# Two low PSUM banks for the output projection and both FFN layers, and the last merged tile added on VectorE

## The chip, the cores and the metric

The kernel runs on one core of one Trainium2 chip. The metric is the device time of one execution in microseconds (us). TensorE (PE) does the matmuls and transposes; VectorE (DVE), ScalarE (ACT) and GpSimd (POOL) do the elementwise work; SyncE (SP) issues most of the DMA loads and stores. TensorE's results land in PSUM, which has eight banks here, each as wide as one 128x512 fp32 tile. TensorE's weight loads stand apart in the profile as PEld.

## The reference

Two batches, `x_prompt` and `x_sample`, both 1024 tokens by 1024 channels, go through one encoder layer with the same weights:

```python
proj = x @ w_in                       # q, k, v of A and of B, gates ga and gb
ya = mixer_a(qa, ka, va) @ w_branch_a # dilated window attention, 12 heads
yb = neighbourhood_attention(qb, kb, vb, rpb) @ w_branch_b
merged = sigmoid(ga + b_gate[0]) * ya + sigmoid(gb + b_gate[1]) * yb
x = layer_norm(alpha * x + merged @ w_out)
hid = square(relu(x @ w_ff1 + b_ff1)) # 4096 wide
x = layer_norm(alpha * x + hid @ w_ff2 + b_ff2)
```

## The kernel before

The program takes the batches one after the other and goes through the same stages for each: transposes of the input and the V columns, q and k and attention A, attention B and the gates, the merge of the two branches, the output projection with the first layer norm, FFN1, FFN2, the second layer norm. Every product of two fp32 matrices is three matmuls: each operand is split into a rounded high part and the low remainder (names that end in `h` and `l`, or 0 and 1), and high x high, high x low and low x high are summed in one bank. One such triple stands on lines L107 to L109, and the subtraction that makes a low part on L103.

A scheduler sets the order of the instructions on each engine from the tiles that they read and write, and from the pools from which the tiles come; the function names and loops of the code alone don't. Each engine then runs its own list strictly in order. A tile waits for the last reader of the tile that had its place before it.

Merge: for each of eight 128-channel tiles `nt` and each half `h` of the tokens, branch A goes into a PSUM tile `py0` and branch B into `py1` (pool `pga`, six banks). VectorE multiplies each by its gate (`sg`, L766), GpSimd adds the two (L767), ScalarE rounds the sum to `bh` (L768), and VectorE takes the low part `bl` (L103).

Output projection: for each half `nh` of the output channels and each half `h` of the tokens, four token tiles `i` take 24 matmuls each, so a group (nh, h) is 96 matmuls in four banks. With nh = 0 the loop over the eight k tiles is outside and the four tiles alternate. `z` is the residual: VectorE adds the finished bank to it (L881), and only then is the bank free. The tiles `wor`, `woh`, `wol` are the projection's weights; `w1t` and `w1b` are the first FFN1 weights, which SyncE loads in the same stretch, and which ScalarE and VectorE split (`oh`, `ol`, and `o` for a piece of `w1b`).

FFN1 runs a Strassen-like scheme in 16 jobs; the first four (`EARLY`) start while the transposes of the second half of the layer norm's output are still coming. Its PSUM tiles are `px`, `pz` and `py`. FFN2 runs the products of a like scheme into four long-lived `px` tiles and short-lived `pt` and `pr` tiles; `acc` is its sum in SBUF. At the end of the first batch VectorE adds the last `px` tiles to `acc`, normalises, and the second batch's input transposes (`pt`, L214) and V products (`psv`) start.

Where the PSUM tiles of before lie: transposes `pt` from the layer norm to FFN2 on banks 0 and 1; the projection's four `pso` on 2, 5, 4, 3; FFN1's and FFN2's `px` on the same four; `pz` and `py`, then `pr`, on 7 and 6. In the merge the last `py0` is on bank 2 and the last `py1` on bank 5.

Of the kernel before, what the change touches and what calls it, by code (L numbers as in the profile page):

```python
# [9 lines left out]
F32 = mybir.dt.float32  # L10
F32R = mybir.dt.float32r
AF = mybir.ActivationFunctionType
ALU = mybir.AluOpType
PSUM = bass.MemoryType.PSUM
# [4 lines left out]
P = 128  # L19
T = 1024  # L20
D = 1024
KT = D // P
# [59 lines left out]
def encoder_kernel(ctx, tc, xs, w_in, b_gate, w_a, w_b, w_out, rpb, ln1_g, ln1_b, w1, b1, w2, b2,  # L82
                   ln2_g, ln2_b, ident_d, rope_d, maska_d, maskb_d, outs):
    nc = tc.nc
# [185 lines left out]
    for b, x in enumerate(xs):  # L270
# [7 lines left out]
        pst = pool("ps_t", 2, space=PSUM)  # L278
# [475 lines left out]
        for nt in range(KT):  # L754
            ns = slice(nt * P, (nt + 1) * P)
            wu = wunit([w_a[:, ns], w_b[:, ns]])
            sg = [sgp.tile([P, T], F32, name=f"sg{s}", tag=f"sg{s}") for s in range(2)]
            for s in range(2):
                nc.sync.dma_start(sg[s], gd[b][s, nt])
                nc.scalar.activation(sg[s], sg[s], AF.Sigmoid)  # L760
            for h in range(2):
                hs = slice(512 * h, 512 * (h + 1))
                py = [pga.tile([P, 512], F32, name=f"py{s}", tag=f"py{s}") for s in range(2)]
                for s, (k0, k1) in enumerate(((0, 2), (2, 6))):
                    mmT(py[s], wu, abt[0][:, :, hs], abt[1][:, :, hs], k0, k1, k0)
                    nc.vector.tensor_tensor(sg[s][:, hs], sg[s][:, hs], py[s], op=ALU.mult)  # L766
                nc.gpsimd.tensor_tensor(sg[0][:, hs], sg[0][:, hs], sg[1][:, hs], op=ALU.add)  # L767
                nc.scalar.copy(mT[h][0][:, nt], sg[0][:, hs])  # L768
                sub(nc.vector, mT[h][1][:, nt], sg[0][:, hs], f(mT[h][0][:, nt]))
        pga.release()  # L770
# [14 lines left out]
        zp = pool("z", 4, side="right")  # L785
        ttp = pool("tt", 2, side="right")
        z0p = pool("z0", 4, side="right")
        pst = pool("ps_t2", 2, space=PSUM)
        pso = pool("ps_o", 4, space=PSUM)

        def split(oh, ol, src, eng):
            nc.scalar.copy(oh, src)  # L792
# [68 lines left out]
        for nh in range(2):  # L861
            wo = []
            for k in range(KT):
                raw = wrw.tile([P, 512], F32, name="wor", tag="wraw")
                nc.sync.dma_start(raw, w_out[k * P:(k + 1) * P, nh * 512:(nh + 1) * 512])
                wh = wop.tile([P, 512], F32R, name="woh", tag="woh")
                wl = wop.tile([P, 512], F32R, name="wol", tag="wol")
                split(wh, wl, raw, nc.vector)
                wo.append((wh, wl))
            for h in range(2):  # L870
                pss = [pso.tile([P, 512], F32, name="pso", tag="pso") for _ in range(4)]
                order = [(k, i) for k in range(KT) for i in range(4)]
                if nh == 1:
                    order.sort(key=lambda o: o[1])
                for k, i in order:
                    cs = slice(i * P, (i + 1) * P)
                    mm3(pss[i], mT[h][0][:, k, cs], mT[h][1][:, k, cs], *wo[k], k == 0, k == KT - 1)
                    if k < KT - 1:
                        continue
                    it = 4 * h + i  # L880
                    nc.vector.scalar_tensor_tensor(zs[it][:, nh], in0=zs[it][:, nh], scalar=ALPHA, in1=pss[i],  # L881
                                                   op0=ALU.mult, op1=ALU.add)
                    if nh == 1:
                        normalise(zs[it])
                        if it > 1:
                            follow(it - 2)
# [20 lines left out]
        sp_ = pool("w1s", 1)  # L907
        c11p = pool("c11", 4)
        psx = pool("ps_x", 4, space=PSUM)
        psy = pool("ps_y", 1, space=PSUM)  # L910
        psz = pool("ps_z", 1, space=PSUM)
        NP = FF // 256
        EARLY = 4

# [11 lines left out]
        def job_a(p, top):  # L926

            o = w1_ops(top, nc.vector)
            px = psx.tile([P, 512], F32, name="px", tag="px")
            prod(px, [t[:, :4] for t in o], xb[1], True)  # L930
            pl, tag = ((psz, "pz"), (psy, "py"))[p % 2 if p < EARLY else 0]
            pz = pl.tile([P, 512], F32, name=tag, tag=tag)
            prod(pz, [t[:, 4:] for t in o], xb[2], True)
            c11 = c11p.tile([P, 512], F32, name="c11", tag="c11")
            nc.scalar.copy(c11, px)  # L935
            nc.vector.tensor_tensor(c11, c11, pz, op=ALU.add)
            return px, c11
# [13 lines left out]
        def job_b(p, top, px, c11):  # L951
            bot = bots.pop(p)
            ss = sp_.tile([P, 4, 4, P], F32, name="ss", tag="ss")
            s2, s1, s3, s4 = (ss[:, i] for i in range(4))
            a11, a12, a21, a22 = top[:, :4], top[:, 4:], bot[:, :4], bot[:, 4:]
            nc.vector.tensor_tensor(s1, a21, a22, op=ALU.add)
            sub(nc.vector, s2, s1, a11)
            sub(nc.vector, s3, a11, a21)
            sub(nc.vector, s4, a12, s2)
            o65 = w1_ops(ss[:, 0:2].rearrange("p i k c -> p (i k) c"), nc.vector)  # L960
            o73 = w1_ops(ss[:, 2:4].rearrange("p i k c -> p (i k) c"), nc.vector)
            o4 = [opq.tile([P, 4, P], F32R, name=f"o4{s}", tag=f"o4{s}") for s in range(2)]
            split(*o4, a22, nc.vector)

            if p + 1 < NP:
                tops[p + 1] = w1_top(p + 1)
                bots[p + 1] = w1_bot(p + 1)
            residual_load(p - EARLY)
            relu2(c11, c11, 2 * p)
            put(p, 1, c11)  # L970
            u2, u3, p5 = (pup.tile([P, 512], F32, name=n, tag=n) for n in ("u2", "u3", "p5"))
            prod(px, [t[:, :4] for t in o65], xb[6], False)
            nc.scalar.copy(u2, px)
            py = psy.tile([P, 512], F32, name="py", tag="py")
            prod(py, [t[:, 4:] for t in o65], xb[5], True)
            nc.scalar.copy(p5, py)
            prod(px, [t[:, :4] for t in o73], xb[7], False)
            nc.scalar.copy(u3, px)
            prod(py, [t[:, 4:] for t in o73], xb[3], False)
            c12, c21, c22, h1, h2, h3, h4 = (htp.tile([P, 512], F32, name="ht", tag="ht") for _ in range(7))  # L980
            nc.vector.tensor_tensor(c12, u2, py, op=ALU.add)
            relu2(c12, c12, 2 * p)
            nc.vector.tensor_tensor(c22, u3, p5, op=ALU.add)
            relu2(c22, c22, 2 * p + 1)
            prod(px, o4, xb[4], False)
            relu2(c21, px, 2 * p + 1)

            put(p, 4, c22)
            put(p, 2, c21)
            nc.vector.tensor_tensor(h1, c12, c22, op=ALU.add)  # L990
            put(p, 5, h1)
            sub(nc.vector, h2, h1, c11)
            put(p, 6, h2)
            sub(nc.vector, h3, c11, c12)
            put(p, 7, h3)
            sub(nc.vector, h4, c21, h2)
            put(p, 3, h4)
# [26 lines left out]
        for p in range(NP):  # L1024
            top = tops.pop(p)
            job_b(p, top, *(early[p] if p < EARLY else job_a(p, top)))
            residual(p - EARLY)
        psz.release()
        psy.release()
        psx.release()  # L1030
        for q in (rsp, htp, pup, opq, opp, awp, c11p, sp_, bop, xbp):
            q.release()
# [19 lines left out]
        w2r = pool("w2r", 2, side="right")  # L1052
        jkp = pool("junk", side="right")
        psx = pool("ps_x", 4, space=PSUM)
        psr = pool("ps_r", 2, space=PSUM)
        nch = NP // 4
        px = [None] * 4

# [5 lines left out]
        for c in range(nch):  # L1064
# [34 lines left out]
            def product(m, t):  # L1099

                if m == 1:
                    px[t] = psx.tile([P, 512], F32, name="px", tag="px")
                if m in (1, 6, 7, 4):
                    ps = px[t]
                else:
                    pl, tag = ((pst, "pt"), (psr, "pr"))[t % 2]
                    ps = pl.tile([P, 512], F32, name=tag, tag=tag)
                cs = slice(t * P, (t + 1) * P)
                for u in range(2):
                    o = ops[m, u]  # L1110
                    for q in range(2):
                        mm3(ps, o[:, 0, q, cs], o[:, 1, q, cs], o[:, 2, q], o[:, 3, q], m not in (6, 7, 4) and u + q == 0,
                            u + q == 2, skip=True)
                for s_ in {1: (0,), 2: (0,), 6: (1,), 5: (1, 3), 3: (1,), 7: (3,), 4: (2,)}[m]:
                    a = acc[s_ // 2][:, t, s_ % 2]
                    nc.vector.tensor_tensor(a, a, ps, op=ALU.add)
                if last and (m == 3 or m == 4 and b + 1 == len(xs)):
                    finish(m == 4, t)
# [9 lines left out]
            if last:  # L1128
                for t in range(4):
                    product(7, t)  # L1130
                    product(4, t)
        psr.release()
        psx.release()
        pst.release()
        for q in (jkp, w2r, hrp, w2a, w2b, padp, ac0p):
            q.release()
        if b + 1 == len(xs):
# [42 lines left out]
```

## Time and profile before

| | before |
|---|---|
| device time, three runs, us | 3073.8, 3064.63, 3077.58 (median 3073.8) |
| profiled execution: time, span, us | 3073.11, 3071.3 |
| PE busy | 2925.7 us, 95% |
| VectorE busy | 1857.7 us, 60% |
| ScalarE busy | 1450.0 us, 47% |
| GpSimd busy | 954.8 us, 31% |
| mean DMA rate over the span | 153 GB/s |

The span is the profiled execution from first to last instruction. Busy time counts an instruction from start to end. TensorE's matmuls overlap: one of 128x512 is shown as 0.39 us, but the next starts 0.23 us after it at the full granted clock. A bracket at the end of a row gives the time for which the engine stood idle before it and the instruction that ended the wait. PEclk is the TensorE clock that was granted, 1.00 for 2.4 GHz and 0.50 for 1.2 GHz.

### The profile page before, as it was taken

To read this page: it belongs to the slowest core of one execution; us is meant where nothing else is said; L and a number is where in the kernel's file an instruction comes from. 1 tells how busy PE (TensorE), PEld (TensorE's weight loads), DVE (VectorE), ACT (ScalarE), POOL (GpSimd) and SP (SyncE) were. 2 spreads that over 40 slices of the span, in tenths; PEclk is the share of its full clock that TensorE was granted. 3 is DMA by queue.
4 is the path that set the end of the run, shared out by engine and by line. 5 is a ranking of instruction groups with operands and counts; after the bars stand their busy time and mean duration, and the time that the engine had idled before them with its cause. 6 is when DMAs were issued, how large, how long until landed. Compare 5 with 4: busy or idle time off the path is not lost. (4 is left out here: it accounts for less than half of the span.)

```text
span 3071.3 us, 39485 instructions
## 1 busy us (share of the span) xinstructions
PE 2925.7 (95%) x13965; PEld 2413.5 (79%) x13965; DVE 1857.7 (60%) x3448; ACT 1450.0 (47%) x2640; POOL 954.8 (31%) x768
## 2 busy tenths in 40 slices
PE   9999999898998999899899999999989999989997
PEld 8887887787776887688797888777878777867886
DVE  2166667545477555888731666685454676558777
ACT  3165755454274554333431656554542745543333
POOL 4665633414014000233242645334140140003332
PEclk9999999999999999999999999999999999999999
DMA  8622235555456547544353222355544565465442
GB/s 254 237 79 80 85 107 154 160 173 154 153 177 226 170 138 258 184 151 138 98 197 109 78 85 76 107 154 163 173 151 159 177 227 164 150 251 167 151 137 82
DMA packets 390662, 471.25 MB, mean 153 GB/s; under 512 B 28424, under 2 KB 270008, under 8 KB 390208
## 3 DMA queue, kind: packets, MB, share of 16 engines
q1 hardware_dynamic: 363968, 430.45, 43.7%
q10 hardware_dynamic: 26496, 38.28, 3.5%
q8 instruction: 110, 1.80, 0.2%
q14 instruction: 88, 0.72, 0.1%
HBM read 321.50 MB, written 147.52 MB: 153 GB/s over the span
## 5 line engine op out<-in xcount | busy, mean ns | idle before, releaser
L107 PE MATMUL pmm<-bh,whi 128*128 128x512 f32 x1152 | 466.1, 405 | 6.8 <-DVE kz L103 4.9
L108 PE MATMUL pmm<-bh,wlo 128*128 128x512 f32 x1152 | 464.0, 403 | 0.0
L109 PE MATMUL pmm<-bl,whi 128*128 128x512 f32 x1152 | 463.1, 402 | 0.0
L103 POOL TENSOR_TENSOR wlo<-wraw,whi 128x512 fp32r<-128x512 f32 (+1 forms) x176 | 225.6, 1294 | 438.9 <-ACT whi L198 383.8
L107 PEld LDWEIGHTS pmm<-bh,whi 128*128 128x128 f32 x1152 | 219.0, 190 | 49.4 <-DVE kz L103 5.9
L400 ACT ACTIVATE smk<-smk,nm 128x256 f32<-128x256 f32 (+4 forms) x320 | 162.3, 508 | 194.7 <-DVE nm L399 176.9
L109 PEld LDWEIGHTS pmm<-bl,whi 128*128 128x128 f32 x1152 | 218.9, 190 | 42.8
L108 PEld LDWEIGHTS pmm<-bh,wlo 128*128 128x128 f32 x1152 | 219.0, 190 | 41.0
L103 POOL TENSOR_TENSOR ts<-rw,rw 128x1024 f32<-128x1024 f32 x12 | 33.7, 2811 | 671.8 <-DMA rw<-in_w_ff_dram 298.2
L792 ACT CAST bh<-hr 128x1024 fp32r<-128x1024 f32 x56 | 58.8, 1050 | 331.2 <-PE px L109 171.5
L103 DVE TENSOR_TENSOR ptl<-pt,pth 128x512 fp32r<-128x512 f32 (+3 forms) x224 | 125.6, 569 | 67.0 <-ACT pth L711 44.2
L107 PE MATMUL psv<-wv,bh 128*128 128x384 f32 (+1 forms) x384 | 138.6, 362 | 1.5 <-ACT wv L295 1.3
L108 PE MATMUL psv<-wv,bl 128*128 128x384 f32 (+1 forms) x384 | 139.2, 363 | 0.3 <-DVE bl L103 0.3
L109 PE MATMUL psv<-wv,bh 128*128 128x384 f32 (+1 forms) x384 | 138.0, 361 | 1.3 <-POOL wv L103 1.2
L103 POOL TENSOR_TENSOR qs<-r,qs 64x512 fp32r<-64x512 f32 x80 | 114.8, 1435 | 62.2 <-ACT qs L423 57.8
L103 DVE TENSOR_TENSOR vt<-psv,vt 128x384 fp32r<-128x384 f32 (+1 forms) x48 | 28.8, 602 | 165.1 <-ACT vt L351 165.1
L792 ACT CAST oh<-ss 128x1024 fp32r<-128x1024 f32 x64 | 67.2, 1053 | 123.2 <-DVE ss L103 93.5
L103 DVE TENSOR_TENSOR bh<-hr,bh 128x1024 fp32r<-128x1024 f32 x56 | 80.9, 1445 | 61.4 <-ACT bh L792 61.1
L198 ACT CAST whi<-wraw 128x512 fp32r<-128x512 f32 (+1 forms) x176 | 97.5, 596 | 42.2 <-DMA wraw<-in_w_in_dram 36.1
L107 PE MATMUL pso<-woh,bh 128*128 128x512 f32 x256 | 104.3, 407 | 12.7 <-DVE sg L766 12.7
L107 PE MATMUL px<-bh,oh 128*128 128x512 f32 x256 | 104.4, 408 | 9.6 <-ACT c L935 4.4
L108 PE MATMUL px<-bh,ol 128*128 128x512 f32 x256 | 104.1, 406 | 4.7 <-DVE ol L103 4.5
(281 smaller groups left out, 8360.2 us busy)
## 6 DMA issues: line engine op xcount, KB each, us to landing
hr<-hidd SPq DMA_DIRECT2D x112, 512.0 KB
hidd<-ht SPq DMA_DIRECT2D x192, 256.0 KB
wraw<-in_w_in_dram SPq DMA_DIRECT2D x144, 256.0 KB
rw<-in_w_ff_dram SPq DMA_DIRECT2D x64, 512.0 KB
w1t<-in_w_ff_dram SPq DMA_DIRECT2D x40, 512.0 KB
gd<-gt ACTq DMA_DIRECT2D x32, 512.0 KB
sg<-gd SPq DMA_DIRECT2D x32, 512.0 KB
w1b<-in_w_ff_dram SPq DMA_DIRECT2D x32, 512.0 KB
```

Source lines behind the costliest of these rows:

```text
L103: eng.tensor_tensor(out, a, b, op=ALU.subtract)
L107: nc.tensor.matmul(out, ah, bh, start=start, stop=False, skip_group_check=skip)
L108: nc.tensor.matmul(out, al, bh, start=False, stop=False, skip_group_check=skip)
L109: nc.tensor.matmul(out, ah, bl, start=False, stop=stop, skip_group_check=skip)
L198: nc.scalar.copy(hi[:, ks], raw[:, :k])
L400: nc.scalar.activation(pr[:, e0:e1], pr[:, e0:e1], AF.Exp, bias=nm, scale=1.0, accum_out=den)
L792: nc.scalar.copy(oh, src)
```

## The change

First, the last merged tile (`nt` = 7) adds its two gated branches on VectorE instead of GpSimd: four instructions in all, two per batch. Second, PSUM is laid out anew from the output projection on. A pool `psl` of two banks, 0 and 1, is opened first and kept until the end of the batch; `low(0)` and `low(1)` are its tiles (`pl0`, `pl1`). They take the projection's token tiles i = 0 and 1, then FFN1's `pz` and `py`, then FFN2's `pr`. The transposes' pool `pst` lies on banks 2 and 3, the projection's two `pso` on 4 and 5, `px` on 4, 7, 6, 5. In the next batch the first transposes lie on banks 2 and 3, which before belonged to `px` tiles and now to short-lived `pt` tiles.

```diff
@@ branch merge
-                nc.gpsimd.tensor_tensor(sg[0][:, hs], sg[0][:, hs], sg[1][:, hs], op=ALU.add)
+                eng = nc.vector if nt == KT - 1 else nc.gpsimd
+                eng.tensor_tensor(sg[0][:, hs], sg[0][:, hs], sg[1][:, hs], op=ALU.add)
@@ output projection
+        psl = pool("ps_l", 1, space=PSUM)
+
+        def low(i):
+            return psl.tile([P, 512], F32, name=f"pl{i}", tag=f"pl{i}")
+
         pst = pool("ps_t2", 2, space=PSUM)
-        pso = pool("ps_o", 4, space=PSUM)
+        pso = pool("ps_o", 2, space=PSUM)
...
-                pss = [pso.tile([P, 512], F32, name="pso", tag="pso") for _ in range(4)]
+                pss = [low(i) if i < 2 else pso.tile([P, 512], F32, name="pso", tag="pso") for i in range(4)]
@@ FFN1
-        psy = pool("ps_y", 1, space=PSUM)
-        psz = pool("ps_z", 1, space=PSUM)
...
-            pl, tag = ((psz, "pz"), (psy, "py"))[p % 2 if p < EARLY else 0]
-            pz = pl.tile([P, 512], F32, name=tag, tag=tag)
+            pz = low(p % 2 if p < EARLY else 0)
...
-            py = psy.tile([P, 512], F32, name="py", tag="py")
+            py = low(1)
@@ FFN2
-        psr = pool("ps_r", 2, space=PSUM)
...
-                    pl, tag = ((pst, "pt"), (psr, "pr"))[t % 2]
-                    ps = pl.tile([P, 512], F32, name=tag, tag=tag)
+                    ps = low(t // 2) if t % 2 else pst.tile([P, 512], F32, name="pt", tag="pt")
...
-        psr.release()
         psx.release()
         pst.release()
+        psl.release()
```

The scheduler makes a new order from this. Up to the end of the branch products of the first batch the order of TensorE is the same. TensorE at the start of the first batch's output projection, before (`py1` is the last branch product, `woh` and `wol` the weights, `bh0` and `bl0` the merged tile of the first half of the tokens):

```order
L109 MATMUL py1_8010<-ab1_7444,whi_7968 128x512
L107 MATMUL pso_8127<-woh_8081,bh0_7502 128x512
L108 MATMUL pso_8127<-woh_8081,bl0_7503 128x512
L109 MATMUL pso_8127<-wol_8082,bh0_7502 128x512
L107 MATMUL pso_8128<-woh_8081,bh0_7502 128x512
```

and now:

```order
L109 MATMUL py1_8010<-ab1_7444,whi_7968 128x512
L107 MATMUL pl0_8130<-woh_8084,bh0_7502 128x512
L108 MATMUL pl0_8130<-woh_8084,bl0_7503 128x512
L109 MATMUL pl0_8130<-wol_8085,bh0_7502 128x512
L107 MATMUL pl1_8131<-woh_8084,bh0_7502 128x512
```

The first tile was on bank 2 and the second on bank 5, both of which the merge had just used; now the two are on banks 0 and 1, and TensorE runs 23 matmuls into these before it turns to banks 4 and 5 (`pso_8132`, `pso_8133`).

VectorE from the end of the merge to the first tiles of the projection, before (`sg` the gates and the merged sum, `ol` and `o41` low parts of FFN1 weights, `z` the residual; `pso_8127` to `pso_8130` are the four banks of the first group):

```order
L766 TENSOR_TENSOR sg1_7979<-sg1_7979,py1_7985 128x512
L766 TENSOR_TENSOR sg0_7978<-sg0_7978,py0_8009 128x512
L103 TENSOR_TENSOR bl0_7503<-sg0_7978,bh0_7502 128x512
L766 TENSOR_TENSOR sg1_7979<-sg1_7979,py1_8010 128x512
L103 TENSOR_TENSOR bl1_7505<-sg0_7978,bh1_7504 128x512
L103 TENSOR_TENSOR ol_8969<-w1t_8966,oh_8968 128x1024
L103 TENSOR_TENSOR ol_9004<-w1t_9001,oh_9003 128x1024
L103 TENSOR_TENSOR o41_9135<-w1b_9119,o40_9134 128x512
L103 TENSOR_TENSOR ol_9039<-w1t_9036,oh_9038 128x1024
L881 SCALAR_TENSOR_TENSOR z_8063<-z_8063,pso_8127 128x512
L881 SCALAR_TENSOR_TENSOR z_8064<-z_8064,pso_8128 128x512
```

and now:

```order
L766 TENSOR_TENSOR sg1_7979<-sg1_7979,py1_7985 128x512
L768 TENSOR_TENSOR sg0_7978<-sg0_7978,sg1_7979 128x512
L766 TENSOR_TENSOR sg0_7978<-sg0_7978,py0_8009 128x512
L103 TENSOR_TENSOR bl0_7503<-sg0_7978,bh0_7502 128x512
L766 TENSOR_TENSOR sg1_7979<-sg1_7979,py1_8010 128x512
L768 TENSOR_TENSOR sg0_7978<-sg0_7978,sg1_7979 128x512
L103 TENSOR_TENSOR bl1_7505<-sg0_7978,bh1_7504 128x512
L103 TENSOR_TENSOR ol_8966<-w1t_8963,oh_8965 128x1024
L103 TENSOR_TENSOR ol_9001<-w1t_8998,oh_9000 128x1024
L103 TENSOR_TENSOR o41_9132<-w1b_9116,o40_9131 128x512
L888 SCALAR_TENSOR_TENSOR z_8066<-z_8066,pl0_8130 128x512
L888 SCALAR_TENSOR_TENSOR z_8067<-z_8067,pl1_8131 128x512
```

The two additions (now L768) stand between the multiplications. The first `z` still stands behind `o41`, the low part of `w1b`; one later `ol` has gone behind two of the `z`. TensorE's second group of 96 begins with the bank that the first `z` sets free, in both orders, and the second batch has the same order here.

VectorE at the end of the first batch, before (`acc` FFN2's sum in its last normalisation, `pt_13628` and `pt_13635` the first transposes of the second batch):

```order
L1116 TENSOR_TENSOR acc1_11457<-acc1_11457,px_13081 128x512
L236 TENSOR_TENSOR acc0_11456<-acc0_11456,bb2_13019 128x1024
L247 SCALAR_TENSOR_TENSOR acc1_11457<-acc1_11457,rs2_13793,bb2_13019 128x1024
L241 BN_AGGR mv_13810<-bst_13811 128x2
L243 TENSOR_SCALAR rs_13803<-mv_13798 128x1
L246 SCALAR_TENSOR_TENSOR acc1_11457<-acc1_11457,mv_13798,g2_13017 128x1024
L240 BN_STATS bst_13823<-acc1_11457 128x6
L103 TENSOR_TENSOR bl0_13604<-pt_13628,bh0_13603 128x4x128
L103 TENSOR_TENSOR bl0_13604<-pt_13635,bh0_13603 128x4x128
```

and now:

```order
L1116 TENSOR_TENSOR acc1_11452<-acc1_11452,px_13073 128x512
L236 TENSOR_TENSOR acc0_11451<-acc0_11451,bb2_13011 128x1024
L103 TENSOR_TENSOR bl0_13596<-pt_13620,bh0_13595 128x4x128
L240 BN_STATS bst_13803<-acc1_11452 128x6
L240 BN_STATS bst_13815<-acc1_11452 128x6
L103 TENSOR_TENSOR bl0_13596<-pt_13627,bh0_13595 128x4x128
L247 SCALAR_TENSOR_TENSOR acc1_11452<-acc1_11452,rs2_13785,bb2_13011 128x1024
L243 TENSOR_SCALAR rs_13795<-mv_13790 128x1
L246 SCALAR_TENSOR_TENSOR acc1_11452<-acc1_11452,mv_13790,g2_13009 128x1024
```

The two `bl0` that free the first two transpose banks have moved ahead of part of the normalisation, but still stand behind the addition of the last `px` and L236.

## Rows read from the trace of the kernel before

**Rows 1.** The page: busy us, share of the span, instructions, by engine.

```profile
PE 2925.7 (95%) x13965; PEld 2413.5 (79%) x13965; DVE 1857.7 (60%) x3448; ACT 1450.0 (47%) x2640; POOL 954.8 (31%) x768
```

**Rows 2.** Waits of TensorE: us in total, times, longest.

```profile
PE pt L107 <- ACT bh L792: 25.8, 3, 12.1
PE pso L107 <- DVE sg L766: 12.7, 4, 5.2
...
PE px L108 <- DVE ol L103: 4.5, 4, 1.1
PE px L107 <- ACT c L935: 4.4, 2, 2.6
...
PE pz L107 <- DVE c L936: 3.3, 2, 2.3
PE py L107 <- DVE c L936: 3.1, 2, 1.6
```

**Rows 3.** Timeline of TensorE, 763 to 796: start, us, line, operation, [idle before].

```profile
763.26 0.39 PE L109 MATMUL py<-ab,whi 128*128 128x512 f32 x1
768.87 0.80 PE L107 MATMUL pso<-woh,bh 128*128 128x512 f32 x1 [5.22 <-DVE sg L766]
...
777.34 0.40 PE L108 MATMUL pso<-woh,bl 128*128 128x512 f32 x1
...
795.52 0.39 PE L107 MATMUL pso<-woh,bh 128*128 128x512 f32 x1
```

**Rows 4.** Windows: stretch, length, engines' busy time, PEclk, DMA share, GB/s.

```profile
768.80:777.30 8.50, 7.29 (x16) 5.28 (x17) 1.99 (x4) 1.24 (x2) 2.11 (x2) 0.50 1.01 339
777.30:788.50 11.20, 11.20 (x51) 9.20 (x50) 2.45 (x2) 2.73 (x3) 0.00 (x0) 1.00 1.11 345
963.20:972.00 8.80, 8.62 (x28) 6.37 (x29) 8.77 (x11) 6.76 (x12) 3.43 (x2) 0.81 0.61 191
1531.30:1542.20 10.90, 7.52 (x28) 6.57 (x29) 10.85 (x15) 4.83 (x10) 8.46 (x6) 0.53 0.72 239
```

**Rows 5.** Timeline of VectorE, 767 to 796.

```profile
767.53 1.28 DVE L766 TENSOR_TENSOR sg<-sg,py 128x512 f32<-128x512 f32 x2
...
773.65 0.69 DVE L103 TENSOR_TENSOR bl<-sg,bh 128x512 fp32r<-128x512 f32 x1 [2.04 <-ACT bh L768]
...
788.53 0.69 DVE L103 TENSOR_TENSOR o<-w1b,o 128x512 fp32r<-128x512 f32 x1 [5.30 <-ACT o L792]
...
793.68 2.05 DVE L881 SCALAR_TENSOR_TENSOR z<-z,pso 128x512 f32<-128x512 f32 x3 [1.72 <-PE pso L109]
```

**Rows 6.** Timelines of GpSimd, ScalarE and SyncE's queue, 768 to 788.

```profile
771.69 1.27 POOL L767 TENSOR_TENSOR sg<-sg,sg 128x512 f32<-128x512 f32 x1 [2.05 <-DVE sg L766]
...
787.87 0.62 ACT L792 CAST o<-w1b 128x512 fp32r<-128x512 f32 x1 [5.91 <-DMA w1b<-in_w_ff_dram]
...
774.37 3.98 SPq L860 DMA_DIRECT2D z<-in_x_prompt_dram  x4
778.39 0.43 SPq L948 DMA_DIRECT2D w1b<-in_w_ff_dram  x1
```

**Rows 7.** The same place in the second batch: TensorE, then VectorE.

```profile
2304.04 0.80 PE L107 MATMUL pso<-woh,bh 128*128 128x512 f32 x1 [5.21 <-DVE sg L766]
...
2323.55 0.69 DVE L103 TENSOR_TENSOR o<-w1b,o 128x512 fp32r<-128x512 f32 x1 [5.24 <-ACT o L792]
...
2327.65 2.05 DVE L881 SCALAR_TENSOR_TENSOR z<-z,pso 128x512 f32<-128x512 f32 x3 [0.66 <-PE pso L109]
```

**Rows 8.** Between the batches: TensorE, VectorE and GpSimd.

```profile
1531.24 0.78 PE L214 MATMUL pt<-ident,xt 128*128 128x128 f32 x4 [4.94 <-DVE acc L1116]
...
1536.10 1.11 PE L214 MATMUL pt<-ident,xt 128*128 128x128 f32 x4 [2.30 <-DVE bl L103]
...
1538.18 2.02 DVE L247 SCALAR_TENSOR_TENSOR acc<-acc,rs,bb 128x1024 f32<-128x1024 f32 x1
...
1535.22 5.85 POOL L103 TENSOR_TENSOR wv<-wvr,wv 128x384 fp32r<-128x384 f32 x4
```

More of the change, by code (lines that the diff above doesn't have):

```diff
@@ L1027, in encoder_kernel @@
             residual(p - EARLY)
-        psz.release()
-        psy.release()
         psx.release()
```

## The prediction

> **What bounds the kernel.** I read the busy times first, then TensorE's waits, then the timelines around the largest waits that the change touches. TensorE is busy 95% of the span [rows 1]: so only what makes it stand still, or run at the lower clock, can shorten the run; a microsecond saved on GpSimd or VectorE counts only if TensorE was waiting for it. Among the waits [rows 2] the reader is to see one that names the changed line's neighbour: the output projection waits four times, 12.7 us in all, for VectorE's multiplication of the gates (L766), 5.2 us at the longest. The largest wait, 25.8 us for `bh` at FFN2's start, has nothing of the change in it: the tiles there have the same number of banks and stand in the same order, so I leave it. The other rows are waits of FFN1 whose order shifts; they return under the rivals.
>
> The place itself is in [rows 3]. The last branch matmul starts at 763.26, the next matmul at 768.87, after 5.22 us of standing still, because bank 2 still holds `py0` and VectorE has not multiplied it (the two multiplications start at 767.53 [rows 5]). After a second, short wait the matmuls crawl: the granted clock from 768.8 to 777.3 is 0.50, that is 1.2 GHz, and 1.00 behind it [rows 4]. The group of 96 ends, and the next begins, at 795.52. From 777.34 (the 17th matmul) to there are 80 matmuls in 18.18 us, so 0.227 us each at full clock. Without any loss the group would take 96 x 0.227 = 21.8 us from 763.49 (763.26 and one step) and end at 785.3. The loss is 10.2 us: two waits of 5.2 and 1.2, and some 3.7 of clock and restart. In the second batch the wait is 5.21 us before 2304.04 [rows 7]; its next group begins 1.84 us after the first `z`, as in the first batch (795.52 less 793.68), at 2329.5. The last branch matmul there is again 5.4 us before 2304.04, so the loss is 2329.5 - 2298.7 - 21.8 = 9.0 us. Both together, 19.2 us, are the most that this part of the change can remove.
>
> **Banks 0 and 1 for the first tiles.** TensorE no longer waits at 763.5: banks 0 and 1 are not used by the merge, and 23 matmuls go into them. Three go to `pso_8132` on bank 4, whose multiplication is long done. Then `pso_8133` on bank 5 needs the multiplication of the last `py1`. It is wanted at 763.49 + 26 x 0.227 = 769.4. VectorE begins the last five steps at 767.53 as before (multiplication, addition, multiplication, `bl0`, multiplication); two multiplications take 1.28 us there [rows 5], so five steps take 3.2 us and end at 770.7, a little later for the rounding on ScalarE between them: 770.9. A wait of 1.5 us remains. I charge no clock for it (it is the nearest to the 1.15 us wait, a part of the 12.7, not the long one); if the clock falls here, add 1.7. The group then ends at 763.5 + 21.8 + 1.5 = 786.8, against 795.5.
>
> **What is late next.** The second group starts with bank 0, and its first matmul needs `z` to have read `pl0`. On VectorE that `z` stands behind `o41`, the low part of `w1b`, in both orders. Before, `o41` started at 788.53 and `z` was ready to run at 793.68, when TensorE had only just finished the first bank (1.72 us of waiting for it) [rows 5]: `o41` cost nothing, hidden behind the slow projection. Now the cover is gone. `o41` waits for ScalarE's cast, which waited 5.91 us for the DMA of `w1b` and started at 787.87 [rows 6]. So `z` can start no sooner than about 788.53 + 0.61 = 789.1, ends at 789.8 (0.68 apiece), and TensorE resumes at 789.9. The new wait is 789.9 - 786.8 = 3.1 us.
>
> Does `w1b` come sooner? SyncE issues it at 778.39, behind four `z` loads that begin at 774.37, which is just when the last `bl` is done (773.65 + 0.69) [rows 5, 6]. With the additions on VectorE that `bl` ends earlier: a GpSimd addition takes 1.27 us [rows 6] and a VectorE step some 0.61, with two handovers less; I get 772.8, 1.5 us sooner. But the DMA engines have a busy share of 1.01 from 768.8 to 777.3 and 1.11 from there to 788.5 [rows 4]: they are full, and `w1b` lands 9.5 us after its issue. I take the arrival as fixed by the bytes ahead of it; if it moves with its issue, each batch gains up to 1.5 us more.
>
> The Trainium skill's page "DMA: Bandwidth & Descriptors", section "Queues, rings and completion order", says that each DMA engine consumes the descriptors of a ring in order. The trace agrees so far as the late landing behind full engines shows it. By that rule the sum stays as it is; without it, it would be up to 3 us lower.
>
> The clock after the new wait: behind a wait of 2.60 us in FFN1 (the longest for `c` [rows 2]) the granted clock was 0.81 over 8.8 us, which costs 8.8 x 0.19 = 1.7 us; behind the 5.2 us wait above it costs 3.7. For 3.1 us I take 2.4, nearer to the first; it could be nothing. So the first batch gains 795.5 - (789.9 + 2.4) = 3.2 us (bounds: 1.9 and 7.1). In the second batch `o41` started at 2323.55 [rows 7], `z` would end at 2324.85, TensorE resumes at 2324.9 after 2.9 us of waiting, and with 2.4 us of clock the gain is 2329.5 - 2327.3 = 2.2 us (0.9 to 6.1). Together 5.4 us, of the 19.2.
>
> **The addition on VectorE.** Four instructions leave GpSimd and four of some 0.61 to 0.69 us come to VectorE. They are inside the chain above; elsewhere VectorE has slack here (it stands idle 5.30 us before `o41`). No term of its own.
>
> **Between the batches.** Before, TensorE had run four transposes, then waited 4.94 us for VectorE's last `px` addition, 1.08 for a weight, 2.30 for `bl` [rows 8], and ran at a clock of 0.53 until 1542.2 [rows 4]. Now banks 2 and 3 are free in time, and the first two transpose tiles run at once. But the third needs `bl0` of the first, which stands behind the last `px` addition and L236: of the same steps, the same end, about 1531.5. So the 4.9 us wait only changes its name; what goes is the 2.30 us wait in the middle, since all four tiles of that stage are done sooner. At its back GpSimd's splits of the weights (5.85 us for four, from 1535.22 [rows 8]) still feed the V products, so part is given back. I take a gain of 2 us, with bounds of 1 us lost (a weight's cast now queues behind a later `bh` on ScalarE) and 5 gained (the whole second wait and half of the clock).
>
> **FFN1 and the rest.** `pz` and `py` had banks 7 and 6, never used by the projection; now they have 0 and 1, which the projection's i = 0 and 1 set free before i = 2 and 3. No wait follows. The order of FFN1 on VectorE shifts by a few places, with the `c` additions a little earlier among the `ht`. No row prices that; its waits in [rows 2] (`ol`, `c` twice, `py` and `pz`: 4.5, 4.4, 3.3, 3.1) sum to 15.3 us, and I let them change by up to 40% either way: 0, with bounds of 6.
>
> **Sum.** 3.2 + 2.2 + 2 + 0 = 7.4 us. The profiled execution took 3073.1 us (span 3071.3), 0.7 below the median of the three runs, 3073.8; so 3065.7 from the one and 3066.4 from the other: **3066**.
>
> **Rivals.**
> 1. *The wait is not handed on.* `w1b` lands before the projection needs `z`, and all 19.2 us go, with the 2 between the batches: 3073.1 - 21.2 = 3052. For it: the loads are issued 1.5 us sooner, and most of the 5.22 us wait surely goes. Against: `w1b` would have to be 3 us sooner while the DMA engines are full.
> 2. *FFN1's order turns against it (the slower side).* The place is the first jobs of FFN1, where TensorE waits for `c`, `ol`, `py`, `pz` behind a VectorE queue. If the shifted order puts these additions behind one `ht` or `ol` more each, the 15.3 us double, and every doubled wait (ten or so) costs a further 1.0 us or so of clock: +25, less the 7.4: 3091. It decides from the point where the new waits exceed 7.4 us, that is half of the present ones again. Against: the `c` additions mostly move forward, not back.
> 3. *Nothing is left.* The 5.4 us earn nothing, because the later weights of FFN1 arrive when they did, and the boundary stays as it was: 3072. For it: the DMA engines are full here, and TensorE's later waits for `ol` are for weights.
>
> **Chances.** The forecast 0.60, with its own range 3058 to 3074; rival 1 0.15; rival 2 0.08; rival 3 0.17. A measurement of this kernel tells a change of about 0.5%, 15.4 us, from none: faster means below 3058.4, slower above 3089.2. Faster: rival 1, and 0.06 of the forecast's lower end: 0.21. Slower: about half of rival 2: 0.04. The rest, 0.75, is within. The range 3052 to 3077 leaves out about half of rival 1 and rival 2: 0.15.
>
> **What would show it.** Right: no wait at the first projection matmul in either batch, a wait of 1 to 2 us some 26 matmuls later, then a wait of about 3 us at the 97th whose releaser is `z`, with VectorE standing before `o41`; the second group starting near 790 and 2325; a wait near 5 us at the third transpose tile between the batches. Wrong: no wait at the 97th matmul (rival 1); FFN1's waits for `c`, `ol`, `py`, `pz` well over 15 us (rival 2); the gain seen at 795 but gone by 1000 (rival 3). A clock that stays at 1.00 behind the new wait would make each batch 2.4 us better.

## The result and the profile after

The changed kernel takes 3053.74 us (median of 5 runs, 3048.26 to 3055.46) against 3067.55 (5 runs, 3064.63 to 3077.58): the ratio is 0.9939, with a 95% interval of 0.9925 to 0.9953. It is faster, by about 0.6%: 18.8 us by the profiled spans, 13.8 by these two medians and 19.7 by the medians of a second set of runs ("changed again" below, 3051.32 against 3070.99). Forecast were 7.4. Its profiled execution took 3054.35 us, with a span of 3052.5.

The page after, to be set beside [rows 1]: TensorE has as many instructions and is busy 9.4 us less, and the span is 18.8 us shorter: so about half of the gain is waiting that has gone, and half is matmuls that take less time, at the full clock. Four instructions have moved from POOL to DVE.

```profile
PE 2916.3 (96%) x13965; PEld 2411.2 (79%) x13965; DVE 1846.7 (60%) x3452; ACT 1450.6 (48%) x2640; POOL 949.3 (31%) x764
```

TensorE's waits, total, times and longest, to be set beside [rows 2]: the wait for the gates (L766) has fallen from 12.7 us in four to 5.3 in two, and a new one, for `z`, has come.

```profile
PE pt L107 <- ACT bh L799: 23.4, 3, 11.6
...
PE pt L214 <- DVE bl L103: 5.6, 2, 5.0
...
PE pso L107 <- DVE sg L766: 5.3, 2, 2.7
...
PE pl L107 <- DVE z L888: 2.1, 2, 1.5
```

TensorE at the first output projection, for [rows 3]:

```profile
765.16 0.40 PE L109 MATMUL py<-ab,whi 128*128 128x512 f32 x1
765.40 0.39 PE L107 MATMUL pl<-woh,bh 128*128 128x512 f32 x1
...
774.17 0.50 PE L107 MATMUL pso<-woh,bh 128*128 128x512 f32 x1 [2.70 <-DVE sg L766]
...
791.84 0.50 PE L107 MATMUL pl<-woh,bh 128*128 128x512 f32 x1 [1.50 <-DVE z L888]
```

The reader is to see three things. The projection begins 0.24 us behind the merge, not 5.6. The 27th matmul waits for bank 5. The 97th, the first of the second group, waits for `z`. From the end of the merge to the 97th it is 791.84 - 765.40 = 26.4 us; before, it was 795.52 - 763.49 = 32.0. VectorE, ScalarE and SyncE's queue name what `z` waits for, as in [rows 5, 6]:

```profile
789.84 0.62 ACT L799 CAST o<-w1b 128x512 fp32r<-128x512 f32 x1 [5.93 <-DMA w1b<-in_w_ff_dram]
...
790.49 0.69 DVE L103 TENSOR_TENSOR o<-w1b,o 128x512 fp32r<-128x512 f32 x1 [5.32 <-ACT o L799]
791.10 1.28 DVE L888 SCALAR_TENSOR_TENSOR z<-z,pl 128x512 f32<-128x512 f32 x2
...
780.65 0.43 SPq L952 DMA_DIRECT2D w1b<-in_w_ff_dram  x1
```

`z` starts the moment `o41` is out of the way, and `o41` waits for `w1b`, 9.2 us after its issue. The windows (PEclk is the third number from the right) show that the clock did not fall in this stretch of the first batch, and fell for 3.4 us behind the 27th matmul in the second:

```profile
768.80:777.30 8.50, 5.80 (x26) 4.47 (x25) 5.86 (x9) 2.39 (x4) 0.00 (x0) 1.00 0.81 285
777.30:788.50 11.20, 11.20 (x51) 9.30 (x50) 2.45 (x2) 2.10 (x2) 0.00 (x0) 1.00 1.09 357
788.50:795.50 7.00, 5.50 (x25) 4.24 (x24) 5.01 (x8) 1.67 (x2) 0.00 (x0) 1.00 0.64 153
2295.20:2298.60 3.40, 3.33 (x8) 2.69 (x9) 1.40 (x3) 0.62 (x1) 0.00 (x0) 0.53 1.01 384
```

In the second batch the 27th and the 97th matmul wait as in the first, and `z` again stands behind `o41`; TensorE, then VectorE:

```profile
2295.27 0.80 PE L107 MATMUL pso<-woh,bh 128*128 128x512 f32 x1 [2.65 <-DVE sg L766]
...
2313.49 0.50 PE L107 MATMUL pl<-woh,bh 128*128 128x512 f32 x1 [0.62 <-DVE z L888]
...
2312.14 0.69 DVE L103 TENSOR_TENSOR o<-w1b,o 128x512 fp32r<-128x512 f32 x1 [5.30 <-ACT o L799]
```

Between the batches, TensorE's answer to [rows 8]: the 4.94 us wait has indeed changed its name only, and the 2.30 us wait behind it has become 0.67.

```profile
1518.83 0.82 PE L214 MATMUL pt<-ident,xt 128*128 128x128 f32 x6
1524.62 1.12 PE L214 MATMUL pt<-ident,xt 128*128 128x128 f32 x4 [4.98 <-DVE bl L103]
1526.41 1.12 PE L214 MATMUL pt<-ident,xt 128*128 128x128 f32 x4 [0.67 <-DVE bl L103]
```

The two projections and the stretch between the batches give some 10 us of the 18.8. The largest part of the rest lies where the prediction did not look: in attention A of the second batch. The windows from the last V product of the second batch to the first matmul of attention B (L704), before and then after:

```profile
1660.80:1961.90 301.10, 293.86 (x1561) 242.80 (x1560) 179.22 (x502) 178.08 (x394) 157.18 (x124) 0.99 0.26 81
```

```profile
1653.10:1948.70 295.60, 292.10 (x1569) 242.85 (x1567) 176.21 (x502) 178.74 (x394) 161.49 (x124) 1.00 0.27 82
```

It is 5.5 us shorter for the same work: TensorE stands idle 3.5 us there instead of 7.2, and is busy 1.8 us less. The waits of TensorE in that stretch, before and then after:

```profile
PE S L511 <- DVE stat L396: 2.3, 2, 1.3
PE pmm L107 <- ACT r L459: 1.9, 1, 1.9
PE po L387 <- ACT pth L527: 1.3, 3, 0.7
PE pt L516 <- ACT smk L400: 1.2, 3, 0.6
```

```profile
PE pmm L107 <- ACT r L459: 1.7, 1, 1.7
PE po L388 <- DVE ptl L103: 1.0, 2, 0.6
```

The edit touches no line of the attention. But the scheduler hands the second batch another order there. Counted row by row over all of the attention and gates, TensorE's order in the second batch differed from that in the first by 1841 rows before, and differs by 10 now. In the first batch attention A took 294.6 us in both kernels.

### The profile page after: what moved, and what is told of

Same layout as the page of the kernel before. It is cut to its first block, busy times and chain, and to the rows that moved or that the text cites. A ratio compares the mean times of both kernels' runs of the same rounds, so it can differ in the third digit from the quotient of the medians.

```text
span 3052.5 us, 39475 instructions
## 1 busy us (share of the span) xinstructions
PE 2916.3 (96%) x13965; PEld 2411.2 (79%) x13965; DVE 1846.7 (60%) x3452; ACT 1450.6 (48%) x2640; POOL 949.3 (31%) x764
## 5 line engine op out<-in xcount | busy, mean ns | idle before, releaser
L107 PE MATMUL px<-bh,oh 128*128 128x512 f32 x256 | 103.2, 403 | 13.8 <-ACT oh L799 10.0
L107 PE MATMUL pl<-bh,oh 128*128 128x512 f32 x256 | 102.2, 399 | 6.0 <-DVE c L940 4.2
```

Of the source, the lines that this page charges most:

```text
L107: nc.tensor.matmul(out, ah, bh, start=start, stop=False, skip_group_check=skip)
```

## The experiments

Each kernel ran in 4 to 12 timed runs beside the kernel before. The table gives each ratio with its interval, and stage lengths in us from the profiled execution: the two output projections (last branch matmul to last projection matmul), attention A of the second batch (as in the windows above), FFN1 of the second batch (last projection matmul to first matmul of FFN2).

| kernel | ratio | projection 1, 2 | attention A, 2nd | FFN1, 2nd | span |
|---|---|---|---|---|---|
| before | | 102.0, 100.7 | 301.1 | 333.0 | 3071.3 |
| before again | 0.9997 (0.9988 to 1.0006) | 101.3, 100.9 | 302.5 | 335.5 | 3070.9 |
| addition only | 0.9982 (0.9972 to 0.9992) | 100.5, 100.0 | 300.9 | 333.2 | 3061.7 |
| low pool second | 0.9996 (0.9987 to 1.0005) | 100.6, 100.3 | 302.1 | 341.1 | 3067.4 |
| changed | 0.9939 (0.9925 to 0.9953) | 96.5, 97.0 | 295.6 | 332.2 | 3052.5 |
| changed again | 0.9941 (0.9922 to 0.996) | 96.4, 95.9 | 295.5 | 335.5 | 3048.4 |
| banks only | 0.9931 (0.9919 to 0.9944) | 96.3, 95.8 | 295.6 | 335.3 | 3044.9 |
| changed, w1b on ScalarE's queue | 0.9928 (0.9913 to 0.9944) | 95.9, 94.3 | 295.6 | 337.1 | 3049.9 |
| six banks, second batch | 0.9969 (0.9958 to 0.998) | 97.2, 93.0 | 295.5 | 343.2 | 3061.8 |
| six banks, both | 1.0001 (0.9989 to 1.0014) | 92.3, 92.4 | 301.4 | 344.0 | 3074.9 |
| changed, old attention order | 0.9993 (0.9982 to 1.0004) | 97.3, 95.9 | 300.9 | 343.0 | 3071.7 |
| banks only, w1b on ScalarE's queue | 0.9911 (0.9897 to 0.9925) | 94.2, 96.1 | 295.6 | 332.8 | 3044.9 |

**The kernel before, again.** No edit.

> The kernel before, unchanged, as a measure of what differs from one execution to the next. Theory 1: of the 18.8 us between the first two profiles only the two output projections (5.5 and 3.7 us) belong to the change; the attention of the second batch (3.6 us), FFN2 (2.3 and 2.1 us) and FFN1 (1.0 and 0.8 us) differ by as much between two executions of one kernel. Then this profile differs from the first one of the same kernel by 2 to 4 us in such stages, while the output projections lose 10 and 9 us again. Theory 2: these stages gain by the change as well. Then this profile repeats the first within about 1 us a stage. Ratio to before 1.000 in both, give or take 0.002.

The projections repeat to 0.7 us. Attention A repeats to 1.4 us, but attention B and the gates of the second batch took 270.5 us here and 266.5 in the first profile, and FFN1 of the first batch 4.4 us less. So a difference of 4 us in those stages says nothing; 6 us in attention A, which lies within 300.9 and 302.5 in every kernel with the old order, is another matter. Theory 1 was wrong to call the whole attention chance.

**The addition only.**

```diff
-                nc.gpsimd.tensor_tensor(sg[0][:, hs], sg[0][:, hs], sg[1][:, hs], op=ALU.add)
+                eng = nc.vector if nt == KT - 1 else nc.gpsimd
+                eng.tensor_tensor(sg[0][:, hs], sg[0][:, hs], sg[1][:, hs], op=ALU.add)
```

> Only the addition of the last merged tile on VectorE; PSUM as before. Theory 1 (the low banks carry the gain): the first projection matmul still waits for the multiplication on bank 2, now 0.6 us later for the addition ahead of it, some 5.8 us, and the clock falls behind it; the second wait may vanish. The two projections lose 9 to 11 us each as before; ratio to before 0.999 to 1.001. Rival (the addition carries it, since the low part of the last tile is ready sooner): ratio 0.995 and the loss at the projection's start halved.

The first projection matmul waits longer, as theory 1 had it, and the second wait is gone:

```profile
767.33 0.80 PE L107 MATMUL pso<-woh,bh 128*128 128x512 f32 x1 [5.87 <-DVE sg L766]
```

Each projection is about 1 us shorter, and the ratio is just below the expected range. The addition alone is worth a little under 0.2%.

**The banks only.** The changed kernel with that addition back on GpSimd.

```diff
-                eng = nc.vector if nt == KT - 1 else nc.gpsimd
-                eng.tensor_tensor(sg[0][:, hs], sg[0][:, hs], sg[1][:, hs], op=ALU.add)
+                nc.gpsimd.tensor_tensor(sg[0][:, hs], sg[0][:, hs], sg[1][:, hs], op=ALU.add)
```

> Only the new PSUM layout; the last addition on GpSimd as before. Theory 1: no wait at the first projection matmul; the 27th waits for the multiplication on bank 5, which now stands behind a low part that waits for GpSimd's addition, some 0.7 us longer than with the addition on VectorE; the wait at the 97th for z is as in the changed kernel (the weights' DMA sets it), so it takes up the 0.7 us in the first batch. Gain of the two projections 8 to 10 us; ratio to before 0.994 to 0.997. Rival (the addition carries it): 0.999 to 1.001.

In the first batch the waits are 2.17 at the 27th and 1.83 at the 97th, in the second 2.79 and 0.67. So the wait at the 27th is not 0.7 us longer than with the addition on VectorE, as was expected (there it is 2.10 to 2.90 us in two profiles), and the projections are as short as in the changed kernel. The whole gain is the layout's; with it the addition's engine makes no difference that can be measured. The ratio is lower than theory 1 allowed, because attention A belongs to the change.

**The low pool second.** The low pool gets banks 2 and 3, the transposes' pool 0 and 1.

```diff
+        pst = pool("ps_t2", 2, space=PSUM)
         psl = pool("ps_l", 1, space=PSUM)
...
-        pst = pool("ps_t2", 2, space=PSUM)
```

> The changed kernel with the two pools in the other order: the transposes' pool on banks 0 and 1, the low pool on banks 2 and 3. Banks are shared between projection, FFN1 and FFN2 as in the change, but the projection's first tile is again on bank 2, which the merge used last. Theory 1: the wait of about 5 us and the clock's fall are back, the projections lose 9 to 11 us each, and the second group waits for nothing, since the late projection hides o41; ratio to before 0.998 to 1.001. Theory 2 (the sharing and the order that follows from it gain in FFN1, FFN2 and attention): about half of the gain stays, ratio 0.996 to 0.998.

```profile
767.53 0.79 PE L107 MATMUL pl<-woh,bh 128*128 128x512 f32 x1 [5.92 <-DVE sg L766]
```

The wait is back, and the gain gone. At the projection it is not that three stages share banks; it is that the first projection tile lies on a bank that the merge didn't just use. But the projections account for only some 8 us of the loss against the changed kernel: the old attention order is back as well (302.1 us), and FFN1 of the second batch takes 341.1 us, for which see the old attention order below.

**The changed kernel, again.** No edit.

> The changed kernel, unchanged, a second time. Its stages so far against the two profiles of the kernel before: the two projections 5 and 4 us shorter, attention of the second batch 564 us against 568 and 573, FFN2 about 2 us shorter in each batch, FFN1 the same. TensorE's order in the second batch's attention is now that of the first batch (10 of 2900 matmuls elsewhere), where before 1841 differ. Theory A (order): attention of the second batch is 563 to 565 us again, as in the first batch. Theory B (variation from one execution to the next): it falls anywhere between 563 and 573. Ratio to before 0.993 to 0.995 in both.

Theory A: attention A 295.5 against 295.6. All of the second batch's attention took 563.4 us.

**w1b on ScalarE's queue.**

```diff
-            nc.sync.dma_start(bot, ...)
+            (nc.scalar if p == 0 else nc.sync).dma_start(bot, ...)
```

> The changed kernel with the load of the first w1b issued by ScalarE's queue, right behind the last bh, instead of SyncE's, where it stands behind four z loads. If the bytes ahead of it in its queue set its arrival, it lands some 4 to 6 us sooner, o41 and the first z no longer wait for it, and the wait at the 97th matmul (1.50 and 0.62 us) falls below 0.7 and to none; w1t lands a little later. If the DMA engines as a whole set it, it lands within 1 us of 789.8 less the shift of the stretch, and the wait stays. Ratio to before 0.992 to 0.995 in either case: this is read from the trace.

ScalarE, its queue and VectorE in the first batch:

```profile
770.54 0.43 ACTq L952 DMA_DIRECT2D w1b<-in_w_ff_dram  x1
...
780.71 1.05 ACT L799 CAST oh<-w1t 128x1024 fp32r<-128x1024 f32 x1 [0.55 <-DMA w1t<-in_w_ff_dram]
781.67 0.61 ACT L799 CAST o<-w1b 128x512 fp32r<-128x512 f32 x1
...
785.44 1.37 DVE L888 SCALAR_TENSOR_TENSOR z<-z,pl 128x512 f32<-128x512 f32 x2 [1.82 <-PE pl L109]
```

The cast no longer waits for `w1b`; `z` waits for TensorE, and the 97th matmul for nothing, in both batches. So what took the old wait's place came from where one load stood, behind four others. What the other queue gave is the earlier issue: 9.3 us behind the merge instead of 15.3, and the cast at 20.4 instead of 24.4. That the load itself is quicker there isn't shown: 11.1 us lie between its issue and its cast, 9.2 in the changed kernel.

**Six banks for the projection, in the second batch, and in both.**

```diff
-        pso = pool("ps_o", 2, space=PSUM)
+        pso = pool("ps_o", 4 if b else 2, space=PSUM)
```

> The changed kernel with four banks in the projection's own pool in the second batch only. The order in the second batch's attention stays that of the changed kernel. The wait at the 97th of the second batch (0.62 us, and what clock it costs) goes. Theory A: attention of the second batch 563 to 565 us, ratio to before 0.992 to 0.994, the same as the changed kernel within 0.001. Theory B gives the same ratio, but with the attention anywhere.

and with 4 in both batches:

> The changed kernel with four banks instead of two in the projection's own pool (banks 4 to 7), so that the second group of 96 starts on fresh banks and needs no z; o41 and w1b as they are. In the attention of the second batch the scheduler's order falls back to that of the kernel before (1837 matmuls differ from the first batch's order). Theory A (the order makes the difference there): the wait at the 97th is gone and the projections are 1 to 2 us shorter than in the changed kernel, but the attention of the second batch is 567 to 573 us again; ratio to before 0.9950 to 0.9975, worse than the changed kernel. Theory B (variation alone): ratio 0.992 to 0.9935, better than the changed kernel by the wait that goes.

Where the projection has six banks, it falls to 92.3 to 93.0 us: the wait at the 27th goes, and of those for `z` 0.4 to 1.0 us are left, behind the 97th. And it is given back. FFN1 of the second batch takes 343 to 344 us. With six banks in both batches the old attention order returns, 301.4 us, and FFN1 and FFN2 of the first batch together take 665.5 us, against 656.9 and 657.4 in the changed kernel. Both ratios are above what either theory said. In FFN1, TensorE of the kernel with six banks in the second batch shows where:

```profile
2451.26 0.79 PE L107 MATMUL px<-bh,oh 128*128 128x512 f32 x1 [12.52 <-ACT oh L799]
```

**The old attention order.** The changed kernel; only in the second batch the V stage's two pools are opened the other way round.

```diff
+        if b:
+            psv = pool("ps_v", 4, space=PSUM)
         pst = pool("ps_t", 2, space=PSUM)
-        psv = pool("ps_v", 4, space=PSUM)
+        if not b:
+            psv = pool("ps_v", 4, space=PSUM)
...
-        psv.release()
-        pst.release()
+        for q in (pst, psv) if b else (psv, pst):
+            q.release()
```

> The changed kernel with one difference: in the second batch the two pools of the V stage are opened in the other order, so the transposes lie on banks 6 and 7 and the V products on 2 to 5. Both pools are closed again before the attention. With it the scheduler gives TensorE in the second batch's attention the order of the kernel before (1 matmul of 2906 elsewhere; against the changed kernel 2046 rows differ), while output projection, FFN1 and FFN2 of the first batch keep the changed order. Theory A (the order of the attention is worth some 6 us): the attention of the second batch takes 567 to 573 us, as in the kernels with that order so far, and the ratio to before rises to 0.9955 to 0.9975. Theory B (those stages differ by chance): 563 to 567 us as in the changed kernel, ratio 0.993 to 0.995.

The window of attention A is that of the kernel before to 0.2 us, and TensorE's busy time in it too:

```profile
1654.70:1955.60 300.90, 293.66 (x1560) 242.72 (x1559) 179.23 (x502) 178.04 (x394) 157.01 (x124) 0.99 0.26 81
```

That settles attention A: same layout of the projection, same shortened projection, old order, old time. In all twelve profiles the old order goes with 300.9 to 302.5 us and the new one with 295.5 to 295.6. What in the old order costs the 6 us was not taken apart. But the ratio is 0.9993, above even theory A's range, since FFN1 of the second batch also lost 8 to 11 us. SyncE, ScalarE and TensorE there:

```profile
2445.93 2.67 SPq L932 DMA_DIRECT2D hidd<-ht  x4
2448.66 0.63 SPq L955 DMA_DIRECT2D w1b<-in_w_ff_dram  x1
...
2453.98 0.62 ACT L802 CAST o<-w1b 128x512 fp32r<-128x512 f32 x1 [4.64 <-DMA w1b<-in_w_ff_dram]
...
2457.01 0.79 PE L107 MATMUL px<-bh,oh 128*128 128x512 f32 x1 [8.58 <-ACT oh L802]
2464.36 0.79 PE L108 MATMUL px<-bh,ol 128*128 128x512 f32 x1 [6.13 <-DVE ol L103]
```

A load of `w1b` stands in SyncE's list behind FFN1's stores (`hidd`), and TensorE waits 8.6 and 6.1 us for what is made of it (`oh` and `ol` are here the parts of `ss`, which VectorE makes of `w1b` and `w1t`). In all four kernels whose second FFN1 takes 341 us or more (low pool second, both with six banks, this one) the fourth `w1b` load stands behind 15 or 16 such stores; in all the others, before and changed among them, it stands behind 10, and none takes over 337.1 us. SyncE's whole FFN1 order in the second batch is the same before and changed. With six banks in both batches that load stands behind 16 stores in the first batch too, instead of 12. No run moves the load alone, so that its place is the cause is read from the traces and not shown by an edit.

**What the runs pointed to.** The banks only, with `w1b` on ScalarE's queue: the two edits above together.

> What the runs so far point to as the fastest: the new PSUM layout with the last addition left on GpSimd, and the load of the first w1b issued by ScalarE's queue. The layout alone gave 0.9931, the changed kernel with that load moved 0.9928. If the two add up (the load's 1 us on the layout alone): 0.991 to 0.993. If the addition on GpSimd takes the load's gain back (a longer wait at the 27th matmul that nothing hides now): 0.993 to 0.9945.

0.9911, 3046.49 us against 3073.09, as expected if the two add up, and the lowest ratio of this study. That it is faster than the changed kernel is likely, not certain: the intervals just meet the first time (0.9925), and overlap with the second set of runs and with the banks only. The 97th matmul waits for nothing in either batch, and the 27th for 2.16 and 2.64 us.

## Why the prediction was right and wrong

From two profiles each of before and changed, as means: the projections give 5.2 and 4.4 us, attention A of the second batch 6.3, the stretch between the batches and the V stage 2.3, FFN2 1.1 and 2.6, and the rest, with FFN1, loses 1.1. Together 20.8 us; the spans differ by 20.7. Forecast were 5.4 for the projections, 2 between the batches and 0 for all else.

- **The chain at the projection held.** No wait at the first matmul, one at the 27th, one at the 97th for `z` behind `o41`. It was predicted that the 97th would start 789.9 - 763.5 = 26.4 us behind the merge in the first batch and 26.2 in the second; measured are 26.4 and 27.0 (2313.49 - 2286.53). Rival 1 fell with that, and the load on ScalarE's queue shows `w1b` to be the reason. That the measured time is near rival 1's 3052 is chance: its mechanism did not occur. The arrival of `w1b` was taken as fixed, and the cast began 24.4 us behind the merge in both kernels (first batch); but the load was issued 14.9 and 15.3 us behind the merge, not 1.5 us sooner as reckoned, so that choice was not put to the test.
- **The clock behind the new wait was mis-sized.** It was charged with 2.4 us in each batch, and measured is nothing. In the first batch the clock stayed at 1.00. In the second it fell behind the 27th (3.4 us at 0.53, some 1.6 us of matmul time), but the 97th still had to wait 0.62 us for `z`, whose start `o41` set: the slower matmuls only shortened that wait. The same holds for the wait at the 27th, which was 2.7 us, not 1.5, because VectorE still waited for the last projection weight's cast. Measured are 9.6 us for the two projections, against 5.4 with the charge and 10.2 without it.
- **Between the batches** 2.3 against 2. The named step is there in both profiles: the wait of 2.30 us has become 0.67. But the whole stretch with the V stage is 0.7 us shorter in one profile of the changed kernel and 4.0 in the other, so that the mean comes so near is in part luck.
- **The step that failed is "FFN1 and the rest ... 0, with bounds of 6".** Everything off the edited lines was taken as one small unknown around FFN1. Within FFN1 the 0 held: its waits for `ol` and `c` fell from 15.3 to 10.5 us, those for `oh` rose from 3.5 to 10.0, and the stage as a whole did not move beyond what two profiles of one kernel differ by. But the attention of the second batch was not in that term at all, although its order on TensorE is a list that could be compared beforehand: 1841 rows that differed from the first batch's order were about to fall to 10, and the first batch's own time for that order, 294.6 us against 301.1, stood in the trace of before. That is 6.3 us, nearly as much as the whole forecast. All that the 0 stood for gave 8.9 us, outside its bounds.
- **Rival 2** named the right stage, with another mechanism: FFN1's order goes with some 6 to 12 us, but through a load in SyncE's list and not through VectorE's additions, and it did not turn in this change. It turned in four of the experiments. **Rival 3** did not occur.
- **Left open:** FFN2 of the second batch is 317.2 to 318.2 us in the kernels with a ratio below 0.997, and 318.5 to 321.1 in the others; no run takes that apart. In the first batch the 1.1 us are less than the 2.1 by which the two profiles of the kernel before differ.

## What to carry to other kernels

Put the first tile of a new stage on a bank (or buffer) that the stage before did not use last, and then look for what the removed wait was hiding: here a load that was issued behind four others, which issuing it from another queue put right. Where a scheduler orders the program, compare the order of every stage, not only around the edit: a changed pool gave the attention of the next batch another order, worth 6 us, and in other variants moved one weight load in FFN1, in kernels whose FFN1 took some 6 to 12 us longer. And where two passes do the same work, the faster pass tells what the other one's order costs.

## What the runs showed of the hardware

Waits of 2.70 and 1.50 us left the clock at 1.00 (windows after, first batch), while a wait of 2.65 us at the same matmul of the second batch was followed by 0.53 for 3.4 us. So two waits of one length, at one place of the program, differ by some 1.6 us of matmul time from one pass to the next. In the kernels with the low pool on banks 0 and 1 the 27th matmul waited thirteen times, 1.37 to 2.90 us: after five of these waits (2.21 to 2.65 us) the clock fell to 0.50, after the others, 2.70, 2.79 and 2.90 among them, it stayed at 1.00. After all eight waits at the first projection matmul, 5.21 to 5.95 us in the kernels that have them, it fell. So behind a wait of 2 to 3 us a clock cost is to be carried as a range that begins at nothing. In attention B and the gates, one kernel's two profiles differed by 4 us in the second batch with the same instruction order.
